# A conformer and latent-attention trunk on one core: scaling order and first taps at the beginning, final norm at the end

## The chip, the cores and the metric

The kernel runs on one core of a Trainium2 chip. The core has TensorE (PE: matrix products and transposes into PSUM; PEld is its weight load), VectorE (DVE), ScalarE (ACT), GpSimd (POOL) and SyncE (SP, which here only issues DMAs). Each engine works through its own instructions in order and waits for others by semaphores. The metric is the time of one execution on the device in microseconds; the time given is the median of several runs.

## The reference, cut to what matters

Two layers over 256 tokens of 2048 channels, all in float32. Layer 0 mixes tokens by a convolution module, layer 1 by latent attention, each is followed by a squared-ReLU MLP, and one RMS norm ends it.

```python
def rms_norm(x, g):
    y = xf * lax.rsqrt(jnp.mean(xf * xf, axis=-1, keepdims=True) + NORM_EPS)
    return (y * g.astype(jnp.float32)).astype(x.dtype)

def conv_module(h, w_pw1, b_pw1, w_dw, b_dw, ln_g, ln_b, w_pw2, b_pw2):
    u = h @ w_pw1 + b_pw1
    a, gate = jnp.split(u, 2, axis=-1)
    u = a * jax.nn.sigmoid(gate)
    u = (causal depthwise convolution of u with w_dw, width 31) + b_dw
    u = jax.nn.silu(layer_norm(u, ln_g, ln_b))
    return u @ w_pw2 + b_pw2

for layer in range(DEPTH):
    h = rms_norm(x, norm_mixer_g[layer])
    x = x + (conv_module(h, ...) if layer % 2 == 0 else mla(h, ...))
    x = x + sq_relu_mlp(rms_norm(x, norm_mlp_g[layer]), mlp_w1[layer], mlp_w2[layer])
return rms_norm(x, final_norm_g)
```

The change touches three places of it: the first `rms_norm` and the first product of `conv_module`, the 31 taps of the first 128 channels, and the last `rms_norm`.

## The kernel before

**Products in two parts.** Every float32 factor is split into a rounded part "hi" and the rest "lo" (`split_half`, L149 to L156). ScalarE rounds (L154: `hi<-raw`), then another engine subtracts (L155: `lo<-raw,hi`). A load of weights ("raw", 1 MB, three buffers) is split in two halves of 128x1024; the hi and lo tiles have six buffers each (`WB`). In the convolution's first product GpSimd does the subtraction, later VectorE does. A product is three matmuls: hi by hi, hi by lo, lo by hi (L482 to L484 in the convolution, L180 to L182 elsewhere).

**The beginning.** The tokens x are loaded to `xs` in four DMAs. VectorE and ScalarE find the mean squares of the two token tiles t, `rsqrt` gives r0. `norm0(n)` scales the 512 channels of block n for both t (two VectorE instructions, L627). `turn0(n)` transposes them on PE (L237, eight transposes), into PSUM tiles of two pools (tr for even n, sum for odd n, two buffers each), and for each 128 channels ScalarE writes the rounded transposed tile (L186) and VectorE its rest (L193). `conv_half(n, h)` splits half h of load n: L154 on ScalarE, L155 on GpSimd. `conv_load(n)` issues load n on SP's queue and waits for a raw buffer, that is for the splits of load n - 3. `conv_mm(c, k0)` is the product of chunk c (128 of the convolution's channels, and as many of the gate) over four blocks of 128 input channels from k0, 24 matmuls; a chunk needs 16 such blocks and two loads. `turn(w_dw ...)` brings the tap weights into place by PE transposes (L276) and VectorE copies (L277). This part stands in `tc.manual_schedule()`: each engine runs its instructions in the order in which the code writes them.

The order written before is: norm0(0), norm0(1), conv_half(0, 0), turn0(0), conv_half(0, 1), conv_load(3), norm0(2), turn0(1), norm0(3), conv_mm(0, 0), turn0(2), both halves of load 1, turn0(3), conv_mm(0, 4), and so on to conv_mm(0, 12).

**The chunks.** For each of 16 chunks `glu` takes a sigmoid on ScalarE (L499) and a product on VectorE (L500) and gives `ub`, 30 columns of padding and 256 tokens. The 31 taps are shared. `pe_taps` does the first three on PE as matmuls with diagonal matrices (L515; the diagonals are made by ScalarE, L506), and ScalarE adds the bias in place (L518). VectorE does the other 28, each one multiply-add into the chunk's PSUM tile (L549). `dve_taps` leaves 16 of them for the next chunk's turn, when VectorE alternates between two chunks. The last two chunks have more taps on PE.

**The end.** `product_A` multiplies by the second MLP matrix in four column blocks of 512. The last block ends with its last three weight loads taken first for token tile 0, then for tile 1, so that tile 0 can be finished while PE works on tile 1. Per tile: `add` (L323) adds the product to `xs`, `prepare` takes squares with their sums on ScalarE (L335), `finish` (L1249) sums the four blocks' squares, takes the inverse root, and scales the four blocks with r and the norm's weights gf in one VectorE instruction each (L1257), each followed by a store issued by SP (L1260).

Of the kernel before, what the change touches and what calls it, by code (L numbers as in the profile page):

```python
# [10 lines left out]
F32 = mybir.dt.float32  # L11
# [3 lines left out]
AF = mybir.ActivationFunctionType  # L15
# [3 lines left out]
P = 128  # L19
D = 2048  # L20
KC = D // P
T = 2
# [12 lines left out]
CHUNK = 64  # L35
HALVES = 2
PAD_CONST = 24
PAD_SMALL = 48
PAD_RIGHT = 48
PAD_KV = 8  # L40
PAD_O = 56
# [31 lines left out]
def trunk_kernel(  # L73
# [54 lines left out]
    def nm(s):  # L128
        uid[0] += 1
        return f"{s}_{uid[0]}"  # L130
# [205 lines left out]

        return ssq, add, prepare

    def product_A(w, k_lo, nk, hi, lo, add, prepare, blocks=range(NNB), due=(), finish=None):


        due = list(due)
        for n in blocks:
            ps = [acc_tile() for _ in range(T)]

            n_end = 3 if finish is not None and n == blocks[-1] else 0
            wjs = []

            def products(u, t):
                for j in range(4):  # L350
                    k = 4 * u + j
                    mm3(ps[t], hi(k, t), lo(k, t), *wjs[u](j), k == 0, k == nk - 1)

            for u in range(nk // 4):
                wjs.append(load_split([rows(w, k_lo + 4 * u, 4, n * NB, NB)], 4))
                if u < nk // 4 - n_end:
                    for j in range(4):
                        k = 4 * u + j
                        for t in range(T):
                            mm3(ps[t], hi(k, t), lo(k, t), *wjs[u](j), k == 0, k == nk - 1)  # L360
                while due:
                    prepare(due.pop(0))
            if n_end:
                for t in range(T):
                    for u in range(nk // 4 - n_end, nk // 4):
                        products(u, t)
                    add(n, ps, t)
                    prepare(n, t)
                    finish(t)
            else:  # L370
                for t in range(T):
                    add(n, ps, t)
                due.append(n)
        while due:
            prepare(due.pop(0))

    def mlp(layer, ssq, next_gain, finish=None):

        with ExitStack() as cx:
            mp = cx.enter_context(tc.tile_pool(name=f"mp{layer}", bufs=1, reuse_waits="tile"))  # L380
            nkh = FF // P // HALVES
            r2 = small.tile([P, T], F32, tag="r2", name=nm("r2"))
            nssq = None
            for hf in range(HALVES):
                hh, hl = [], []
                for g in range(nkh // 4):
                    ps = [acc_tile() for _ in range(4)]
                    c0 = (hf * nkh + 4 * g) * P
                    for u in range(KC // 4):
                        wj = load_split([rows(mlp_w1[layer], 4 * u, 4, c0, NB)], 4)  # L390
                        for j in range(4):
                            k = 4 * u + j
                            wh, wl = wj(j)
                            for b in range(4):
                                bs = slice(b * P, (b + 1) * P)

                                nc.tensor.matmul(ps[b], wh[:, bs], xhl(k), start=k == 0, stop=False)  # L397
                                nc.tensor.matmul(ps[b][:, :S], wl[:, bs], xh(k), start=False, stop=k == KC - 1)  # L398
                    gh = mp.tile([P, 4, S], F32R, tag="gh", name=nm("gh"), bufs=nkh // 4)
                    gl = mp.tile([P, 4, S], F32R, tag="gl", name=nm("gl"), bufs=nkh // 4)  # L400
                    for b2 in range(2):
                        v = mp.tile([P, 2, S], F32, tag="v", name=nm("v"), bufs=2)
                        for b in range(2):
                            o = ps[2 * b2 + b]
                            nc.scalar.activation(v[:, b, :], o[:, S:], AF.Copy)  # L405
                            nc.vector.tensor_tensor(v[:, b, :], o[:, :S], v[:, b, :], op=ALU.add)
                        nc.vector.scalar_tensor_tensor(out=v, in0=v, scalar=0.0, in1=v, op0=ALU.max, op1=ALU.mult)
                        bs = slice(2 * b2, 2 * b2 + 2)
                        nc.scalar.activation(gh[:, bs, :], v, AF.Copy)
                        nc.vector.tensor_tensor(gl[:, bs, :], v, gh[:, bs, :].bitcast(F32), op=ALU.subtract)  # L410
                    hh.append(gh)
                    hl.append(gl)
                if hf == 0:
                    r = rms_rstd(ssq, NNB, D, "n")
                    nc.vector.tensor_tensor(r2, r, r, op=ALU.mult)
                nssq, add, prepare = residual_stage(hf == HALVES - 1, next_gain, r2)
                product_A(
                    mlp_w2[layer],
                    hf * nkh,
                    nkh,  # L420
                    lambda k, t: hh[k // 4][:, k % 4, t * P : (t + 1) * P],
                    lambda k, t: hl[k // 4][:, k % 4, t * P : (t + 1) * P],
                    add,
                    prepare,
                    finish=(lambda t: finish(nssq, t)) if finish is not None and hf == HALVES - 1 else None,
                )
            return nssq


    with ExitStack() as cx:  # L430
# [36 lines left out]
        def conv_split(n):  # L467
            conv_half(n, 0)
            conv_half(n, 1)
# [14 lines left out]
                    nc.tensor.matmul(o, wl[:, bs], xh(k), start=False, stop=k == KC - 1)  # L484

        pss, ubs, pcs, cas, cts = {}, {}, {}, {}, {}
        n_pe = lambda c: PE_TAPS[c % 4] + {KC - 2: PE_MORE[0], KC - 1: PE_MORE[1]}.get(c, 0)
        rest = lambda c: {KC - 2: REST[1], KC - 1: 0}.get(c, REST[0])
        tap = lambda c, w: w_dw[:, w * KC + c : w * KC + c + 1]

# [18 lines left out]
        def pe_taps(c, dgs):  # L509

            pc = pcs[c] = sum_tile()[:, :S]
            for w in range(n_pe(c)):
                if w == len(dgs):
                    dgs.append(diag(c, w))
                nc.tensor.matmul(pc, dgs[w], ubs[c][:, w : w + S], start=w == 0, stop=w == n_pe(c) - 1)  # L515
            left[c] = list(range(n_pe(c), W))
            if c < KC - 1:
                nc.scalar.activation(pc, pc, AF.Identity, bias=b_dw[:, c : c + 1])  # L518
            else:

                pcs[c], last_sum[:] = acc_tile()[:, :S], [pc]

# [7 lines left out]
        def dve_tap(c):  # L530
            w = left[c].pop(0)
            out = pcs[c]
            if last_sum and c == KC - 1:
                if w == n_pe(c):
                    nc.vector.tensor_scalar(
                        out, ubs[c][:, w : w + S], scalar1=tap(c, w), scalar2=b_dw[:, c : c + 1],
                        op0=ALU.mult, op1=ALU.add,
                    )
                    return
                if not left[c]:  # L540
                    half = cv2.tile([P, S], F32, tag="half", name=nm("half"), bufs=1)
                    nc.vector.scalar_tensor_tensor(
# [60 lines left out]
        with tc.manual_schedule():  # L603
# [30 lines left out]
                    to_T(xn, 4 * n + 2 * j, xh, xl, g_mix[0], sum_tile() if n % 2 else None)  # L634


            norm0(0)
            norm0(1)
            conv_half(0, 0)
            turn0(0)  # L640
            conv_half(0, 1)
            conv_load(3)
            pss[0] = [acc_tile() for _ in range(2)]
            norm0(2)
            turn0(1)
            norm0(3)
            conv_mm(0, 0)
            turn0(2)
            conv_split(1)
            turn0(3)  # L650
            conv_mm(0, 4)
            conv_load(4)
            turn(vecs2, vecs2_rows)
            for i in range(4):
                turn(w_dw[:, i * NW : (i + 1) * NW], w_rows[i])
            conv_split(2)
            conv_mm(0, 8)
            conv_mm(0, 12)
            dgs = [diag(0, w) for w in range(n_pe(0))]
            fills = []  # L660
            for c in range(1, KC + 1):
                n = UC * c
# [582 lines left out]
    with tc.tile_pool(name="fin", bufs=1, reuse_waits="tile") as fp:  # L1245
        gf = fp.tile([P, D], F32, name="gf")
        nc.scalar.dma_start(gf, final_norm_g.rearrange("(a n) -> a n", a=1).partition_broadcast(P))

        def finish(ssq, t):  # L1249
            ms = small.tile([P, 1], F32, tag="msf", name=nm("ms"))  # L1250
            nc.vector.tensor_reduce(ms, ssq[:, t, :], axis=AX.X, op=ALU.add)
            nc.vector.tensor_scalar(ms, ms, scalar1=1.0 / D, scalar2=None, op0=ALU.mult)
            r = rsqrt(ms, 1, EPS, "f")
            for n in range(NNB):
                sl = slice(n * NB, (n + 1) * NB)
                ob = xs[:, t, sl]
                nc.vector.scalar_tensor_tensor(  # L1257
                    out=ob, in0=ob, scalar=r, in1=gf[:, sl], op0=ALU.mult, op1=ALU.mult
                )
                nc.sync.dma_start(out[0, t * P : (t + 1) * P, sl], ob)  # L1260

        mlp(1, ssq, None, finish)


_INS = [
# [23 lines left out]
```

## Time and profile before

| what | value |
|---|---|
| median of 3 runs | 2031.42 us (2030.94 to 2032.25) |
| the profiled execution | 2031.51 us |
| its span, first to last instruction | 2029.7 us |
| TensorE busy | 1997.2 us (98%) |
| VectorE, ScalarE, GpSimd busy | 1227.8, 964.5, 174.0 us |
| first product of the convolution (L482) | 15.22 us from the start of the span |
| end of PE's last matmul (wait of L323 ends) | 2020.2 us |
| store issues after it | 2024.41, 2025.07, 2025.73, 2026.40 us |

Times in timelines are microseconds from the start of the span. A row of the timeline has the start, the duration, the engine, the line, the operation, what it writes and reads, and in brackets the idle time of the engine before it and who ended that. "x4" means that four alike were merged. Neighbouring instructions of an engine overlap a little, so the step from one start to the next is shorter than a duration.

### The profile page before, as it was taken

To read this page: it belongs to the slowest core of one execution; us is meant where nothing else is said; L and a number is where in the kernel's file an instruction comes from. 1 tells how busy PE (TensorE), PEld (TensorE's weight loads), DVE (VectorE), ACT (ScalarE), POOL (GpSimd) and SP (SyncE) were. 2 spreads that over 40 slices of the span, in tenths; PEclk is the share of its full clock that TensorE was granted. 3 is DMA by queue.
4 is the path that set the end of the run, shared out by engine and by line. 5 is a ranking of instruction groups with operands and counts; after the bars stand their busy time and mean duration, and the time that the engine had idled before them with its cause. 6 is when DMAs were issued, how large, how long until landed. Compare 5 with 4: busy or idle time off the path is not lost.

```text
span 2029.7 us, 28001 instructions
## 1 busy us (share of the span) xinstructions
PE 1997.2 (98%) x11150; PEld 1749.3 (86%) x11150; DVE 1227.8 (60%) x1858; ACT 964.5 (48%) x1364; POOL 174.0 (9%) x101
## 2 busy tenths in 40 slices
PE   7999999999999999999999899999999999999998
PEld 7999888888888888888898898888888888888886
DVE  5999866665544465555446675665554455565454
ACT  5444665544433354444445564554443334454442
POOL 5887400000000000000000000000000000000000
PEclk9999999999999999999999999999999999999999
DMA  7555355665565666655555335566655566655653
GB/s 235 167 167 166 123 188 174 200 187 187 193 200 187 191 191 193 193 187 188 187 169 171 105 125 168 187 205 188 191 197 192 189 198 192 189 187 190 200 192 104
DMA packets 243267, 367.59 MB, mean 181 GB/s; under 512 B 15416, under 2 KB 89792, under 8 KB 242880
## 3 DMA queue, kind: packets, MB, share of 16 engines
q1 hardware_dynamic: 242400, 364.68, 56.8%
q8 instruction: 87, 1.43, 0.3%
q10 hardware_dynamic: 736, 1.12, 0.2%
q14 instruction: 44, 0.36, 0.1%
HBM read 363.68 MB, written 2.10 MB: 180 GB/s over the span
## 4 chain that ended last, share of the span: by engine, by line
PE 95%; DVE 3%; ACT 1%; issue 0%; DMA 0%; SPq 0%; DVEq 0%; ACTq 0%
PE acc L397 23%; PE acc L180 16%; PE acc L181 16%; PE acc L182 16%; PE acc L398 12%; PE acc L482 3%; PE acc L484 3%; PE acc L483 3%; PE sum L515 1%; PE tr L237 1%; DVE lo L155 1%; DMA xs<-in_x 0%; ACT hi L154 0%; PE acc L1011 0%; PE acc L1012 0%
## 5 line engine op out<-in xcount | busy, mean ns | idle before, releaser
L155 DVE TENSOR_TENSOR lo<-raw,hi 128x1024 fp32r<-128x1024 f32 (+1 forms) x628 | 755.6, 1206 | 682.7 <-ACT hi L154 669.8
L154 ACT ACTIVATE hi<-raw 128x1024 fp32r<-128x1024 f32 (+1 forms) x696 | 722.8, 1046 | 790.2 <-PE acc L181 453.8
L397 PE MATMUL acc<-xt,hi 128*128 128x512 f32 x2048 | 710.6, 390 | 0.0
L398 PE MATMUL acc<-xt,lo 128*128 128x256 f32 x2048 | 577.7, 282 | 0.0
L397 PEld LDWEIGHTS acc<-xt,hi 128*128 128x128 f32 x2048 | 384.3, 188 | 80.5
L180 PE MATMUL acc<-hi,gh 128*128 128x512 f32 x1024 | 398.6, 389 | 0.0
L182 PE MATMUL acc<-lo,gh 128*128 128x512 f32 x1024 | 398.4, 389 | 0.0
L181 PE MATMUL acc<-hi,gl 128*128 128x512 f32 x1024 | 398.4, 389 | 0.0
L398 PEld LDWEIGHTS acc<-xt,lo 128*128 128x128 f32 x2048 | 387.1, 189 | 0.1
L182 PEld LDWEIGHTS acc<-lo,gh 128*128 128x128 f32 x1024 | 192.2, 188 | 40.2
L180 PEld LDWEIGHTS acc<-hi,gh 128*128 128x128 f32 x1024 | 192.2, 188 | 40.0
L181 PEld LDWEIGHTS acc<-hi,gl 128*128 128x128 f32 x1024 | 192.2, 188 | 39.3
L549 DVE SCALAR_TENSOR_TENSOR sum<-ub,w_dw,sum 128x256 f32<-128x256 f32 x402 | 167.6, 483 | 4.9 <-ACT sum L518 2.9
L155 POOL TENSOR_TENSOR lo<-raw,hi 128x1024 fp32r<-128x1024 f32 x68 | 161.9, 2404 | 57.7 <-ACT hi L154 57.7
L482 PE MATMUL acc<-xt,hi 128*128 128x256 f32 x512 | 147.4, 288 | 0.0
L484 PE MATMUL acc<-xt,lo 128*128 128x256 f32 x512 | 143.1, 280 | 0.4 <-POOL lo L155 0.4
L483 PE MATMUL acc<-xt,hi 128*128 128x256 f32 x512 | 143.1, 280 | 0.0
L483 PEld LDWEIGHTS acc<-xt,hi 128*128 128x128 f32 x512 | 96.3, 188 | 0.6 <-DVE xt L193 0.2
L484 PEld LDWEIGHTS acc<-xt,lo 128*128 128x128 f32 x512 | 96.2, 188 | 0.6 <-POOL lo L155 0.6
L482 PEld LDWEIGHTS acc<-xt,hi 128*128 128x128 f32 x512 | 96.3, 188 | 0.4
L918 POOL MEMSET pad_kv<- 128x8 f32 x1 | 0.1, 105 | 772.6 <-PE acc L182 772.6
L405 ACT ACTIVATE v<-acc 128x256 f32<-128x256 f32 x128 | 46.4, 381 | 25.3 <-PE acc L398 25.3
(215 smaller groups left out, 1772.8 us busy)
## 6 DMA issues: line engine op xcount, KB each, us to landing
raw<-in_mlp_w SPq DMA_DIRECT2D x256, 1024.0 KB, 5.2
raw<-in_conv_w_pw SPq DMA_DIRECT2D x64, 512.0 KB, 5.1
raw<-in_conv_w_pw SPq DMA_DIRECT2D x16, 1024.0 KB, 5.2
raw<-in_mla_w_o SPq DMA_DIRECT2D x16, 1024.0 KB, 5.3
raw<-in_mla_w_kv_up SPq DMA_DIRECT2D x8, 1024.0 KB, 5.6
raw<-in_mla_w_in SPq DMA_DIRECT2D x8, 576.0 KB, 3.7
raw<-in_mla_w_in SPq DMA_DIRECT2D x4, 1024.0 KB, 5.6
raw<-in_mla_w_q_up SPq DMA_DIRECT2D x16, 256.0 KB, 3.3
```

The lines of the kernel that those rows point to most:

```text
L154: nc.scalar.activation(hi, raw[:, js, :], AF.Copy)
L155: eng.tensor_tensor(lo, raw[:, js, :], hi.bitcast(F32), op=ALU.subtract)
L180: nc.tensor.matmul(ps, sh, mh, start=start, stop=False)
L181: nc.tensor.matmul(ps, sl, mh, start=False, stop=False)
L182: nc.tensor.matmul(ps, sh, ml, start=False, stop=stop)
L397: nc.tensor.matmul(ps[b], wh[:, bs], xhl(k), start=k == 0, stop=False)
L398: nc.tensor.matmul(ps[b][:, :S], wl[:, bs], xh(k), start=False, stop=k == KC - 1)
L405: nc.scalar.activation(v[:, b, :], o[:, S:], AF.Copy)
L482: nc.tensor.matmul(o, wh[:, bs], xh(k), start=k == 0, stop=False)
L483: nc.tensor.matmul(o, wh[:, bs], xl(k), start=False, stop=False)
L484: nc.tensor.matmul(o, wl[:, bs], xh(k), start=False, stop=k == KC - 1)
L549: nc.vector.scalar_tensor_tensor(out=out, in0=ubs[c][:, w : w + S], scalar=tap(c, w), in1=pcs[c], op0=ALU.mult, op1=ALU.add)
```

## The change

At the beginning, all four `norm0` are written ahead of everything else; the first half of load 1 is split before conv_mm(0, 0) and `turn0(2)`, the second half between `turn0(2)` and `turn0(3)`; the tap weights' turns come one conv_mm later. Chunk 0 has no taps on PE: VectorE does all 31, the first with the bias. At the end, after the first weight load of the last column block, a new function `before` sums the squares of the first three blocks into `part` and multiplies these blocks of `xs` by the norm's weights. `finish` then adds only the last block's squares, multiplies the last block by the weights while ScalarE takes the root, and scales the four blocks by the inverse root alone: blocks 0 and 2 on VectorE with stores from SP's queue, 1 and 3 on ScalarE with stores from its own queue. `PAD_SMALL` makes room for the additional small tiles.

```diff
-PAD_SMALL = 48
+PAD_SMALL = 32
...
+                if u == 0 and n_end:
+                    before()
...
-        n_pe = lambda c: PE_TAPS[c % 4] + {KC - 2: PE_MORE[0], KC - 1: PE_MORE[1]}.get(c, 0)
+        n_pe = lambda c: 0 if c == 0 else PE_TAPS[c % 4] + {KC - 2: PE_MORE[0], KC - 1: PE_MORE[1]}.get(c, 0)
...
-            if c < KC - 1:
+            if 0 < c < KC - 1:
                 nc.scalar.activation(pc, pc, AF.Identity, bias=b_dw[:, c : c + 1])
-            else:
+            elif c:
...
-            if last_sum and c == KC - 1:
-                if w == n_pe(c):
-                    nc.vector.tensor_scalar(
-                        out, ubs[c][:, w : w + S], scalar1=tap(c, w), scalar2=b_dw[:, c : c + 1],
-                        op0=ALU.mult, op1=ALU.add,
-                    )
-                    return
+            if c in (0, KC - 1) and w == n_pe(c):
+                nc.vector.tensor_scalar(
+                    out, ubs[c][:, w : w + S], scalar1=tap(c, w), scalar2=b_dw[:, c : c + 1],
+                    op0=ALU.mult, op1=ALU.add,
+                )
+                return
+            if c == KC - 1:
...
-            norm0(0)
-            norm0(1)
+            for n in range(NNB):
+                norm0(n)
             conv_half(0, 0)
             turn0(0)
             conv_half(0, 1)
             conv_load(3)
             pss[0] = [acc_tile() for _ in range(2)]
-            norm0(2)
             turn0(1)
-            norm0(3)
+            conv_half(1, 0)
             conv_mm(0, 0)
             turn0(2)
-            conv_split(1)
+            conv_half(1, 1)
             turn0(3)
             conv_mm(0, 4)
             conv_load(4)
             turn(vecs2, vecs2_rows)
+            conv_mm(0, 8)
             for i in range(4):
                 turn(w_dw[:, i * NW : (i + 1) * NW], w_rows[i])
             conv_split(2)
-            conv_mm(0, 8)
             conv_mm(0, 12)
-            dgs = [diag(0, w) for w in range(n_pe(0))]
+            dgs = []
...
+        def gained(t, n):
+            sl = slice(n * NB, (n + 1) * NB)
+            nc.vector.tensor_tensor(xs[:, t, sl], xs[:, t, sl], gf[:, sl], op=ALU.mult)
+
         def finish(ssq, t):
-            ms = small.tile([P, 1], F32, tag="msf", name=nm("ms"))
-            nc.vector.tensor_reduce(ms, ssq[:, t, :], axis=AX.X, op=ALU.add)
-            nc.vector.tensor_scalar(ms, ms, scalar1=1.0 / D, scalar2=None, op0=ALU.mult)
-            r = rsqrt(ms, 1, EPS, "f")
...
+            nc.vector.tensor_scalar(v, ssq[:, t, n : n + 1], scalar1=1.0 / D, scalar2=part[t], op0=ALU.mult, op1=ALU.add)
+            nc.scalar.activation(w, v, AF.Sqrt)
+            nc.vector.tensor_tensor(xs[:, t, sl], xs[:, t, sl], gf[:, sl], op=ALU.mult)
+            nc.vector.reciprocal(y, w)
+            nc.vector.scalar_tensor_tensor(out=q, in0=y, scalar=v, in1=y, op0=ALU.mult, op1=ALU.mult)
+            nc.vector.tensor_scalar(q, q, scalar1=-0.5, scalar2=1.5, op0=ALU.mult, op1=ALU.add)
+            nc.vector.tensor_tensor(y, y, q, op=ALU.mult)
             for n in range(NNB):
-                sl = slice(n * NB, (n + 1) * NB)
-                ob = xs[:, t, sl]
-                nc.vector.scalar_tensor_tensor(
-                    out=ob, in0=ob, scalar=r, in1=gf[:, sl], op0=ALU.mult, op1=ALU.mult
-                )
-                nc.sync.dma_start(out[0, t * P : (t + 1) * P, sl], ob)
+                ob = xs[:, t, n * NB : (n + 1) * NB]
+                if n % 2:
+                    nc.scalar.activation(ob, ob, AF.Copy, scale=y)
+                else:
+                    nc.vector.tensor_scalar(ob, ob, scalar1=y, scalar2=None, op0=ALU.mult)
+                (nc.scalar if n % 2 else nc.sync).dma_start(out[0, t * P : (t + 1) * P, n * NB : (n + 1) * NB], ob)
+
+        part = []
+
+        def before(ssq):
+            for t in range(T):
+                m = small.tile([P, 1], F32, tag="msp", name=nm("msp"))
+                nc.vector.tensor_reduce(m, ssq[:, t, : NNB - 1], axis=AX.X, op=ALU.add)
+                nc.vector.tensor_scalar(m, m, scalar1=1.0 / D, scalar2=EPS, op0=ALU.mult, op1=ALU.add)
+                part.append(m)
+                for n in range(NNB - 1):
+                    gained(t, n)
+
+        mlp(1, ssq, None, finish, before)
```

More of the change, by code (lines that the diff above doesn't have):

```diff
@@ L337, in residual_stage, with product_A @@
         return ssq, add, prepare
-    def product_A(w, k_lo, nk, hi, lo, add, prepare, blocks=range(NNB), due=(), finish=None):
+    def product_A(w, k_lo, nk, hi, lo, add, prepare, blocks=range(NNB), due=(), finish=None, before=None):
         due = list(due)
@@ L375, in product_A, with mlp @@
             prepare(due.pop(0))
-    def mlp(layer, ssq, next_gain, finish=None):
+    def mlp(layer, ssq, next_gain, finish=None, before=None):
         with ExitStack() as cx:
@@ L425, in mlp @@
                     finish=(lambda t: finish(nssq, t)) if finish is not None and hf == HALVES - 1 else None,
+                    before=lambda: before(nssq),
                 )
@@ L1253, in finish @@
-            r = rsqrt(ms, 1, EPS, "f")
-            for n in range(NNB):
-                sl = slice(n * NB, (n + 1) * NB)
-                ob = xs[:, t, sl]
-                nc.vector.scalar_tensor_tensor(
-                    out=ob, in0=ob, scalar=r, in1=gf[:, sl], op0=ALU.mult, op1=ALU.mult
-                )
-                nc.sync.dma_start(out[0, t * P : (t + 1) * P, sl], ob)
-        mlp(1, ssq, None, finish)
+            n = NNB - 1
+            sl = slice(n * NB, (n + 1) * NB)
+            v = small.tile([P, 1], F32, tag="msf", name=nm("ms"))
@@ new lines, in finish @@
+            w = small.tile([P, 1], F32, tag="wsf", name=nm("ws"))
+            y = small.tile([P, 1], F32, tag="ysf", name=nm("ys"))
+            q = small.tile([P, 1], F32, tag="qsf", name=nm("qs"))
+            nc.vector.tensor_scalar(v, ssq[:, t, n : n + 1], scalar1=1.0 / D, scalar2=part[t], op0=ALU.mult, op1=ALU.add)
+            nc.scalar.activation(w, v, AF.Sqrt)
+            nc.vector.tensor_tensor(xs[:, t, sl], xs[:, t, sl], gf[:, sl], op=ALU.mult)
+            nc.vector.reciprocal(y, w)
```

## The prediction

> **What bounds the kernel now.** I read the page first: busy time by engine, then the chain that ended last.
>
> ```profile
> PE 1997.2 (98%) x11150; PEld 1749.3 (86%) x11150; DVE 1227.8 (60%) x1858; ACT 964.5 (48%) x1364; POOL 174.0 (9%) x101
> PE 95%; DVE 3%; ACT 1%; issue 0%; DMA 0%; SPq 0%; DVEq 0%; ACTq 0%
> ```
>
> TensorE (PE) is busy for 1997.2 of 2029.7 us, so an edit pays only where it moves PE: in the 32.5 us of gaps, or in PE work that goes away. The timeline puts the gaps that matter here in two places: the first 23 us, and the 9.5 us after the last matmul. Then the timeline of the start (start, duration, engine, line, what came before it):
>
> ```profile
> 12.43 1.68 DVE L627 TENSOR_SCALAR xn<-xs,y 128x512 f32<-128x512 f32 x4
> 13.84 2.49 POOL L155 TENSOR_TENSOR lo<-raw,hi 128x1024 fp32r<-128x1024 f32 x1 [12.46 <-ACT hi L154]
> 15.06 1.66 DVE L193 SCALAR_TENSOR_TENSOR xt<-tr,vecs,xt 128x256 fp32r<-128x256 f32 x4 [0.95 <-PE sum L237]
> 15.60 0.38 PE L483 MATMUL acc<-xt,hi 128*128 128x256 f32 x1
> 16.39 0.39 PE L484 MATMUL acc<-xt,lo 128*128 128x256 f32 x1 [0.40 <-POOL lo L155]
> 16.64 0.48 DVE L627 TENSOR_SCALAR xn<-xs,y 128x512 f32<-128x512 f32 x1
> 16.78 2.59 POOL L155 TENSOR_TENSOR lo<-raw,hi 128x1024 fp32r<-128x1024 f32 x1 [0.45 <-ACT hi L154]
> 17.03 2.63 DVE L627 TENSOR_SCALAR xn<-xs,y 128x512 f32<-128x512 f32 x1
> 19.71 0.98 PE L237 MATMUL tr<-ident,xn 128*128 128x128 f32 x7 [0.35 <-DVE xn L627]
> 21.76 1.29 PE L237 MATMUL sum<-ident,xn 128*128 128x128 f32 x8 [1.07 <-DVE xn L627]
> 22.81 0.37 PE L482 MATMUL acc<-xt,hi 128*128 128x256 f32 x1
> ```
>
> The reader should see one thing above all. A scaling (L627) takes 0.48 us, each starting 0.40 after the last. The one at 17.03 took 2.63, ending 0.29 after GpSimd's split (16.78 + 2.59 = 19.37). So these two exclude each other. And GpSimd, which asked at 16.78 in the middle of the scaling of 16.64, went ahead of the next scaling, although that followed at once.
>
> **The change, start.** All eight scalings now precede VectorE's first L193. Nothing delays GpSimd: its first split waits for ScalarE's rounding (L154), which waits for a DMA, not for VectorE. So I replay the rows with the rule just read (times from the start of the span):
> - Scalings 1 to 4: 12.43 to 14.1 as before. GpSimd asks at 13.84 and goes ahead of scaling 5, which waits for 13.84 + 2.49 = 16.33 and ends 0.29 later, 16.62. Scaling 6 starts 0.08 before that end, 16.54.
> - Split 2 asks at 16.78, as before, again inside a scaling (6). Taking the step from the scaling's start to the split's end from the rows (19.37 - 16.64 = 2.73), it ends at 19.27; scaling 7 ends at 19.56, scaling 8 asks at 19.48.
> - Split 3 is the moved one (conv_half(1, 0)). ScalarE ends its four L186 at 18.0, rounds in 1.07, so it is ready at 19.2 and waits behind split 2. It asks inside scaling 7 (port effectively taken at 19.08) and goes ahead of scaling 8: end 19.08 + 2.73 = 21.81. Scaling 8 ends at 22.1.
> - First L193 at 22.0; L483 stood 0.54 after it (15.06, 15.60), so it runs at 22.56 instead of 15.60: **6.96 us late**. PE is in order, so everything is behind it.
>
> Given back: PE's waits between 15.60 and 22.81 vanish, as splits and scalings are then long done: for the split 15.60 to 16.39 less one step of 0.12, 0.67; for the scalings 0.57 and 1.48 (the step lengths around 19.71 and 21.76, less 0.11 a transpose). 6.96 - 2.72 = **+4.2 us**. The moved ScalarE roundings cost nothing: split 4 then ends near 33, and the third quarter's products only begin after 34; without that cover it would be a split of 2.4 us.
>
> The stall also costs clock. The next rows are stretches in the attention stage (length, busy us and instructions per engine, granted clock, DMA share):
>
> ```profile
> 1123.20:1126.60 3.40, 3.40 (x31) 3.40 (x30) 3.37 (x7) 1.12 (x2) 0.00 (x0) 1.00 0.15 45
> 1126.60:1130.00 3.40, 1.90 (x17) 1.67 (x16) 2.11 (x11) 1.19 (x5) 0.00 (x0) 1.00 0.68 154
> 1130.00:1133.40 3.40, 3.40 (x18) 3.40 (x18) 2.34 (x7) 1.36 (x2) 0.00 (x0) 0.50 0.02 5
> ```
>
> A stretch of 3.4 us in which PE was busy 56% was followed by half clock for a fully busy 3.4 us. A stall of 7 us holds such a stretch whatever its phase, so products start again at half clock: 0.213 us a step (18 matmuls in the row of half clock against 31 in the first, and the 14 warm-up transposes at 9.60 took 3.25) against 0.117. If a stretch under 56% busy does not raise it, half clock lasts 1.9 to 5.3 us of work and loses half, 0.95 to 2.65. On this profile's phase (its clock record steps where stretches end, here at 20.65, 24.07, 27.48; the one to 24.07 would be 44% busy) 23 products lose 2.2. Bounds: 0 and 2.65; I take **+2.0**, near this phase.
>
> The Trainium skill (TensorE: Matmul & The Clock Gate, Part 1) says a whole free-running window of about 3.4 us of sustained activity is needed to release the gate; by that rule the loss is an estimated 1.7 to 3.4 us and the sum some 0.5 larger. The trace agrees with the length, and does not show what a window busy at 44% does.
>
> **First chunk's taps.** Gone from PE: the six matmuls of three taps.
>
> ```profile
> 34.11 0.28 PE L484 MATMUL acc<-xt,lo 128*128 128x256 f32 x1
> 34.23 1.47 PE L515 MATMUL sum<-ub,dg 128*128 128x256 f32 x6
> 35.35 0.47 PE L482 MATMUL acc<-xt,hi 128*128 128x256 f32 x1
> ```
>
> 34.11 to 35.35 less one step: **-1.1 us**. VectorE does 15 taps instead of 12 before the next chunk, 3 x 0.53 = 1.6, but no longer waits 2.25 for L518; it then idled 3.5 us for the sigmoid, which hides it. Without that slack the 1.6 would count. Later chunks leave VectorE 0.6 to 0.8 idle and PE none, so PE's shift stays. The w_dw turns moved past conv_mm(0, 8): five turns took 25.80 to 27.14, and one of their waits for a copy goes: **-0.2** (0 to -0.4). Load 4 on SP's queue waits for split 4 (33 instead of 27.6), for a rounding needed after 40: nothing.
>
> **The end.** The weights' six early multiplications (0.69 each, row L410) and four small steps, 4.8 us, fall where VectorE splits 1.23 of every 2.72 us and ScalarE waits for PE to free one of six halves, so a split is five halves (13 us) ahead: nothing; 4.8 uncovered. The last column block:
>
> ```profile
> 2023.63 2.74 DVE L1257 SCALAR_TENSOR_TENSOR xs<-xs,y,gf 128x512 f32<-128x512 f32 x4
> 2026.40 0.33 SPq L1260 DMA_DIRECT2D out<-xs  x1
> 2026.50:2027.00 0.50, 0.00 (x0) 0.00 (x0) 0.00 (x0) 0.00 (x0) 0.00 (x0) 0.50 1.09 369
> ```
>
> The new chain saves two small steps and pays 0.61 of multiplication under a root of 0.42: 0.2 earlier. The first piece is ready after 0.48 instead of 0.75, so its store issues at 23.95 instead of 24.41. ScalarE's pieces cost 0.63 each (row L335) and its issues 0.44 (ACTq rows at the start), so the last issue is at 25.2 instead of 26.40. But the stores already fill the DMA engines (share 1.09), 1 MB in 3.1 us: the end moves with the first store and a little denser queue. **-0.7** (0 if the stores pack worse, -1.2 if the last issue decides).
>
> **Sum.** +4.2 +2.0 -1.1 -0.2 -0.7 = +4.2. The profiled execution took 2031.51 (span 2029.7 and 1.8 around it), 0.1 over the median 2031.42, so about 2035.7.
>
> **Rivals.**
> - *VectorE keeps the port through its eight scalings.* For it: GpSimd asks only once, 0.2 before scaling 5. Against: the row of 17.03. Scalings end at 15.7, split 1 at 18.0; L484 then waits 1.65 longer, the later waits (2.05) go: -0.4 -0.2 -1.1 -0.7 = -2.4, **2029.1**. This is the case of not slower; it decides if scaling 5 is 0.48 long.
> - *Scaling 8 slips in before split 3.* For it: they ask within 0.05 us of each other's release. Against: so did 17.03 and 16.78. L483 at 20.4: 4.8 - 2.7 = +2.1, clock 0 to 1.7, the rest -2.0: +0.1 to +1.8, **2032.5**.
> - *The clock does not fall, or rises at 24.07.* 0 to 0.7 instead of 2.0: +2.2 to +2.9, **2034.1**. Against: the rows of 1126.60 and 1130.00.
> - *Half clock lasts a further window (1.7), or the stall feeds a second one:* +6, **2037.5** or more. Nothing in the rows asks for it.
>
> **Chances.** Forecast 0.62, clock kept 0.12, VectorE first 0.12, slip 0.08, longer half clock 0.06. Range: I leave out VectorE first and the last (0.18), so from the slip's lower end, less 0.4 by which single runs lie under the median, 2031.2, to the forecast's upper bounds, 4.2 + 2.65 - 1.1 and no other gain, 2037.3. A change under 0.2% (4.1 us) is about what a measurement of this kernel can't tell from none: the bound, 2035.5, cuts the forecast's own range (2034.3 to 2037.3), some 0.7 of it above: 0.62 x 0.7 + 0.06 = 0.50 slower. Faster needs 2027.3, which all savings together at their best (-2.4, with the end at -1.2 and the turns at -0.4: -3.1) miss: 0.04. Same: 0.46.
>
> **What would show it.** Scaling 5 near 2.6 us and 7 or 8 again; first L193 near 22.0 and L483 near 22.6; product steps of 0.213 after it; no L515 before chunk 1; the first products of chunk 1 some 6 us later than before, chunk 2's some 5; last store issue near 1.2 earlier relative to the last matmul, the end 0.7. Eight scalings of 0.48 in a row, or L193 before 18, would make it wrong.

## The result, and the profile after

| | before | changed |
|---|---|---|
| median of 19 runs | 2031.95 us | 2036.03 us |
| range of the runs | 2030.94 to 2033.14 | 2033.26 to 2036.92 |
| profiled execution, its span | 2031.51, 2029.7 | 2036.42, 2034.6 |

The changed kernel is slower by a ratio of 1.0018 (95% interval 1.0011 to 1.0024). The medians differ by 4.1 us, the profiled executions by 4.9. Some lines moved by three: L485 to L487 in the changed kernel are L482 to L484 before, L630 is L627, L502 is L499.

First the timeline of the start in the changed kernel, VectorE and GpSimd, then PE (start, duration, engine, line; rows of a kind are merged differently from stretch to stretch, so a row of scalings can cover others that follow):

```profile
12.53 9.55 DVE L630 TENSOR_SCALAR xn<-xs,y 128x512 f32<-128x512 f32 x8
...
13.93 2.50 POOL L155 TENSOR_TENSOR lo<-raw,hi 128x1024 fp32r<-128x1024 f32 x1 [12.55 <-ACT hi L154]
14.12 2.98 DVE L630 TENSOR_SCALAR xn<-xs,y 128x512 f32<-128x512 f32 x2
16.71 2.60 POOL L155 TENSOR_TENSOR lo<-raw,hi 128x1024 fp32r<-128x1024 f32 x1 [0.28 <-ACT hi L154]
17.03 2.57 DVE L630 TENSOR_SCALAR xn<-xs,y 128x512 f32<-128x512 f32 x1
17.03 5.05 DVE L630 TENSOR_SCALAR xn<-xs,y 128x512 f32<-128x512 f32 x2
19.27 2.52 POOL L155 TENSOR_TENSOR lo<-raw,hi 128x1024 fp32r<-128x1024 f32 x1
22.00 0.86 DVE L193 SCALAR_TENSOR_TENSOR xt<-tr,vecs,xt 128x256 fp32r<-128x256 f32 x2
22.52 0.58 PE L486 MATMUL acc<-xt,hi 128*128 128x256 f32 x1 [7.01 <-DVE xt L193]
...
23.33 0.41 PE L486 MATMUL acc<-xt,hi 128*128 128x256 f32 x1
23.55 0.41 PE L487 MATMUL acc<-xt,lo 128*128 128x256 f32 x1
...
27.43 1.03 PE L237 MATMUL tr<-ident,xn 128*128 128x128 f32 x8
28.30 1.04 PE L237 MATMUL sum<-ident,xn 128*128 128x128 f32 x8
29.09 0.37 PE L485 MATMUL acc<-xt,hi 128*128 128x256 f32 x1
```

Eight scalings of 0.48 us, 0.40 apart, would take 3.3; they take 9.55. The fifth starts at 14.12, just after GpSimd's first split began at 13.93, and it and the sixth last 2.98 together; the seventh takes 2.57, and with the eighth 5.05. So the fifth, the seventh and the eighth are the slow ones, and each ends 0.3 us after one of GpSimd's three splits. (What the two engines cannot use at the same time is called the port, here and in the prediction.) PE waits 7.01 for that L193 and then steps 0.21 a matmul (23.33 to 23.55) until 27.2.

Then the stretches between the clock's steps (length, busy us and instructions of PE, PEld, DVE, ACT, POOL, granted clock, DMA share):

```profile
13.52:16.93 3.41, 1.98 (x17) 1.78 (x16) 3.41 (x4) 3.13 (x8) 2.72 (x2) 1.00 0.73 217
16.93:20.35 3.42, 0.00 (x0) 0.00 (x0) 3.42 (x3) 2.11 (x5) 3.42 (x2) 1.00 0.96 273
20.35:23.76 3.41, 1.24 (x6) 1.24 (x6) 3.41 (x6) 0.00 (x0) 1.44 (x1) 0.50 1.02 325
23.76:27.18 3.42, 3.42 (x18) 3.42 (x18) 1.45 (x4) 0.00 (x0) 0.00 (x0) 0.50 1.06 328
27.18:30.59 3.41, 3.41 (x32) 3.41 (x32) 1.66 (x4) 2.53 (x6) 0.00 (x0) 1.00 0.05 15
```

The idle stretch (16.93 to 20.35) is followed by half clock; the stretch to 23.76, 36% busy, did not raise it; the fully busy one to 27.18 did.

Last, the end of the changed kernel (the last block of token tile 1):

```profile
2025.70 0.75 DVE L323 SCALAR_TENSOR_TENSOR xs<-acc,r,xs 128x512 f32<-128x512 f32 x1 [4.17 <-PE acc L182]
...
2028.80 1.33 ACT L1273 ACTIVATE xs<-xs,ys 128x512 f32<-128x512 f32 x2 [1.11 <-DVE ys L1269]
2028.80 0.88 DVE L1275 TENSOR_SCALAR xs<-xs,ys 128x512 f32<-128x512 f32 x2
2029.31 0.81 SPq L1276 DMA_DIRECT2D out<-xs  x2
2029.55 0.95 ACTq L1276 DMA_DIRECT2D out<-xs  x2
```

And one half microsecond after them, in the columns of the stretches above:

```profile
2031.50:2032.00 0.50, 0.00 (x0) 0.00 (x0) 0.00 (x0) 0.00 (x0) 0.00 (x0) 0.50 1.09 356
```

All four stores are issued within 1.2 us (2029.31 to 2029.55 + 0.95), and the DMA engines are full after them (share 1.09), as they were before.

The same work in both traces shows where the 4.9 us lie:

| landmark | before | changed | difference | of which new |
|---|---|---|---|---|
| products of block 4 begin | 22.81 | 29.09 | +6.28 | +6.28 |
| sigmoid of chunk 0 | 33.03 | 39.19 | +6.16 | -0.12 (turns) |
| sigmoid of chunk 1 | 45.54 | 50.39 | +4.85 | -1.31 (taps) |
| sigmoid of chunk 15 | 225.57 | 229.92 | +4.35 | -0.50 |
| start of the last adds of MLP 0's third block | 998.48 | 1002.84 | +4.36 | 0 |
| first add after the attention | 1267.73 | 1273.17 | +5.44 | +1.08 |
| last L323 | 2020.26 | 2025.70 | +5.44 | 0 |
| end of the span | 2029.69 | 2034.61 | +4.92 | -0.52 (end) |

### The profile page after: what moved, and what is told of

It reads as the page before. It is cut to its first block, busy times and chain, and to the rows that moved or that the text cites. A ratio compares the mean times of both kernels' runs of the same rounds, so it can differ in the third digit from the quotient of the medians.

```text
span 2034.6 us, 27980 instructions
## 1 busy us (share of the span) xinstructions
PE 1997.4 (98%) x11144; PEld 1750.8 (86%) x11144; DVE 1233.5 (61%) x1863; ACT 965.8 (47%) x1364; POOL 174.1 (9%) x101
## 4 chain that ended last, share of the span: by engine, by line
PE 95%; DVE 3%; ACT 1%; issue 1%; DMA 0%; SPq 0%; ACTq 0%; DVEq 0%
PE acc L399 23%; PE acc L182 16%; PE acc L180 16%; PE acc L181 16%; PE acc L400 12%; PE acc L486 3%; PE acc L485 3%; PE acc L487 3%; PE sum L518 1%; PE tr L237 1%; DVE lo L155 1%; DMA xs<-in_x 0%; ACT hi L154 0%; PE acc L1014 0%; PE tr L1097 0%
## 5 line engine op out<-in xcount | busy, mean ns | idle before, releaser
L486 PE MATMUL acc<-xt,hi 128*128 128x256 f32 x512 | 144.2, 282 | 7.0 <-DVE xt L193 7.0
L485 PE MATMUL acc<-xt,hi 128*128 128x256 f32 x512 | 148.0, 289 | 0.0
L487 PE MATMUL acc<-xt,lo 128*128 128x256 f32 x512 | 143.9, 281 | 0.0
L486 PEld LDWEIGHTS acc<-xt,hi 128*128 128x128 f32 x512 | 97.4, 190 | 7.6 <-DVE xt L193 7.2
L485 PEld LDWEIGHTS acc<-xt,hi 128*128 128x128 f32 x512 | 97.3, 190 | 0.4
L487 PEld LDWEIGHTS acc<-xt,lo 128*128 128x128 f32 x512 | 97.2, 190 | 0.0
```

Source lines behind the costliest of these rows:

```text
L485: nc.tensor.matmul(o, wh[:, bs], xh(k), start=k == 0, stop=False)
L486: nc.tensor.matmul(o, wh[:, bs], xl(k), start=False, stop=False)
```

## The experiments

Each kernel was timed beside the kernel before on the same chip, whose medians there were 2031.87 (first four), 2032.19 (next four) and 2031.68 (last three). The changed kernel was not among them: "under the changed kernel" compares bare medians, and taking each against the kernel before that ran beside it moves these differences by up to 0.3 us. The code shown is cut to the lines that matter.

**The order alone.** The kernel before with the changed order of the beginning, nothing else.

```diff
-            norm0(0)
-            norm0(1)
+            for n in range(NNB):
+                norm0(n)
...
+            conv_half(1, 0)
             conv_mm(0, 0)
```

> The kernel before with the new order of the beginning alone (scalings first, the moved split halves, the tap weights' turns later); the taps of chunk 0 and the end as before. Theory (GpSimd goes ahead of waiting scalings, PE stalls, clock falls): scalings 5, 7 and 8 take about 2.6 us, first L193 at 22.0, L483 at 22.5, chunk 0's sigmoid 6 us later than before; +5.5 to +6.5 us over before. Rival (the order costs little, the slower time comes from the taps or the end): within 1 us of before.

Measured: 2037.17 us (2034.59 to 2038.09), ratio 1.0023 (1.0014 to 1.0032), +5.3 us, 0.2 short of the range expected. The loss is the order's, and the order alone is 1.1 slower than the whole change. Its profiled execution took 2035.84 and shows another path, the rival that the prediction called the slip, though not for the reason given there. DVE and GpSimd in it:

```profile
16.52 0.87 DVE L627 TENSOR_SCALAR xn<-xs,y 128x512 f32<-128x512 f32 x2
17.06 2.52 POOL L155 TENSOR_TENSOR lo<-raw,hi 128x1024 fp32r<-128x1024 f32 x1 [0.76 <-ACT hi L154]
17.31 2.56 DVE L627 TENSOR_SCALAR xn<-xs,y 128x512 f32<-128x512 f32 x1
19.79 1.65 DVE L193 SCALAR_TENSOR_TENSOR xt<-tr,vecs,xt 128x256 fp32r<-128x256 f32 x4
37.13 0.48 ACT L499 ACTIVATE sg<-acc,vecs 128x256 f32<-128x256 f32 x1 [1.10 <-PE acc L484]
```

Split 2 asked at 17.06 instead of 16.71, when scaling 7 was already running, so only the eighth waited for it, and L193 begins at 19.79. In this execution the record of the granted clock first rises at 15.09, not 13.52, so PE's first transposes were slower and ScalarE's rounding for split 2 came later. The other profiles bear this out: in the ten in which the work up to split 2 is the same, it starts 4.18 us after the first scaling where the clock first rose at 12.2 to 13.5 us (six), 4.35 in the kernel before (13.83), and 4.53 to 4.65 where it rose at 14.7 to 15.3 (three). The sigmoid of chunk 0 (last row) is +4.1 over before instead of +6.2. So the race between the second split and the seventh scaling has two outcomes some 2 us apart. The changed kernel's 19 runs lie in two groups, 6 from 2033.26 to 2034.43 and 13 from 2035.75 to 2036.92; that these are the two outcomes fits, but is not shown, as no execution of the lower group has been profiled.

**The taps alone, and the end alone.**

```diff
-        n_pe = lambda c: PE_TAPS[c % 4] + {KC - 2: PE_MORE[0], KC - 1: PE_MORE[1]}.get(c, 0)
+        n_pe = lambda c: 0 if c == 0 else PE_TAPS[c % 4] + {KC - 2: PE_MORE[0], KC - 1: PE_MORE[1]}.get(c, 0)
```

> The kernel before with chunk 0's 31 taps on VectorE alone. Theory: PE loses six matmuls, VectorE's 1.6 us more is hidden by its wait for the next sigmoid: -1.1 us (-0.7 to -1.8, as the profile after gained some 0.5 more over the later chunks). Rival (VectorE is the bound of the chunks, the three taps come back at the end of them): 0 to +1.6 us.

Measured: 2030.27 us (2029.46 to 2032.49), ratio 0.9992 (0.9984 to 1.0001), -1.6 us. The sign by the timing is just short of sure; the trace shows the mechanism: the sigmoids of chunks 0 and 1 are 11.20 us apart instead of 12.51, with no wait of PE between. So -1.31 at once, 1.12 for the matmuls and 0.19 at the change between shapes.

```profile
32.92 0.47 ACT L499 ACTIVATE sg<-acc,vecs 128x256 f32<-128x256 f32 x1 [4.61 <-PE acc L484]
44.12 0.47 ACT L499 ACTIVATE sg<-acc,vecs 128x256 f32<-128x256 f32 x1 [6.05 <-PE acc L484]
```

> The kernel before with the new end alone. Theory: -0.5 us, the stores' transfer rate sets the end, the early multiplications are hidden. Rival 1 (the last store's issue sets the end): -1.7 us. Rival 2 (the early multiplications hold up the splits): above 0.

```diff
+                if u == 0 and n_end:
+                    before()
...
-                nc.sync.dma_start(out[0, t * P : (t + 1) * P, sl], ob)
+                (nc.scalar if n % 2 else nc.sync).dma_start(out[0, t * P : (t + 1) * P, n * NB : (n + 1) * NB], ob)
```

Measured: 2030.95 us (2030.57 to 2032.95), ratio 0.9996 (0.9987 to 1.0005), -0.9 us by the medians, which the interval does not tell from nothing and which alone excludes neither rival. The trace does: the last matmul is 8.96 us before the end of the span, against 9.47, so -0.5 and not -1.7; and from the first add after the attention to the last L323 both kernels take 752.53 us, so the early multiplications hold nothing up.

**All but the order.** The changed kernel with the old order of the beginning (between these lines all is as before the change).

```diff
-            for n in range(NNB):
-                norm0(n)
+            norm0(0)
+            norm0(1)
             conv_half(0, 0)
...
+            norm0(2)
             turn0(1)
-            conv_half(1, 0)
+            norm0(3)
             conv_mm(0, 0)
```

> The changed kernel with the old order of the beginning. Theory (the parts add up): -1.1 - 0.5 = -1.6 us against before, some 6 us faster than the changed kernel. Rival (the parts need each other): not faster than before.

Measured twice: 2029.56 us, ratio 0.9988 (0.998 to 0.9997), and beside the last kernels 2030.56, ratio 0.999 (0.9981 to 0.9999). The parts other than the order gain 1.1 to 2.3 us, and taking the order back makes the changed kernel 5.5 to 6.5 faster.

> The same kernel as all_but_order, beside two_forms on one chip: 2029.5 us, -1.5 to -3 against before.

The second came out 1.0 above the figure expected and 0.4 short of the gain's near bound, so single medians here are good to about 1 us. Part of that can be seen in the two profiles of this one kernel: the attention (from the last adds of MLP 0's third block to the first add after it) takes 269.20 us in one, with half clock for two stretches, and 270.40 in the other, with half clock for three.

**The stall filled.** 60 transposes that nothing reads, while PE waits.

```diff
             conv_half(1, 0)
+            keep_warm(ident, 60, warm_pt)
             conv_mm(0, 0)
```

> The changed kernel with 60 transposes of the identity on PE between turn0(1)'s transposes and conv_mm(0, 0): 60 x 0.11 = 6.6 us, from 15.1 to some 21.7, into a tile that nothing reads. They end before L483 can run (22.5), so they add no wait. Theory (the stall also costs clock): the products start again at 0.117 a step, chunk 0's sigmoid comes 2.2 us earlier than in the profile after; -1.8 to -2.2 us against the changed kernel, +2 against before. Rival (the clock costs nothing): equal to the changed kernel, +4 against before.

Measured: 2033.82 us (2033.11 to 2034.41), ratio 1.0008 (1.0 to 1.0017): 2.2 under the changed kernel, and all its runs lie in a range of 1.3 us. In its timeline the scalings and L193 are where they were, and the matmuls step 0.12:

```profile
12.51 9.61 DVE L631 TENSOR_SCALAR xn<-xs,y 128x512 f32<-128x512 f32 x8
15.20 6.71 PE L220 MATMUL acc<-ident 128*128 128x128 f32 x60
22.57 0.39 PE L487 MATMUL acc<-xt,hi 128*128 128x256 f32 x1 [0.53 <-DVE xt L193]
22.79 0.28 PE L488 MATMUL acc<-xt,lo 128*128 128x256 f32 x1
22.91 0.28 PE L486 MATMUL acc<-xt,hi 128*128 128x256 f32 x1
37.13 0.47 ACT L503 ACTIVATE sg<-acc,vecs 128x256 f32<-128x256 f32 x1 [3.96 <-PE acc L488]
```

The sigmoid of chunk 0 is 2.06 earlier than in the changed kernel (39.19). Useless work on PE saves 2 us: this stall costs its length and, besides, the clock.

**The splits held back.** GpSimd copies a column of the eighth scaling's result first, which makes its first split wait (`PAD_SMALL` is 24, for the additional tile).

```diff
+            held = small.tile([P, 1], F32, tag="held", name="held", bufs=1)
+            nc.gpsimd.tensor_copy(held, xn[:, 1, D - 1 : D])
             conv_half(0, 0)
             turn0(0)
```

> The changed kernel in which GpSimd first copies one column of the eighth scaling's result, so that its first split waits for all scalings: the order that the change describes, in fact. Theory (the port is the only cause of the start's loss): eight scalings of 0.48, first L193 at 15.7, first split 15.8 to 18.2, L484 at 18.3, the products of block 4 at 22.4; -0.4 -0.2 -1.1 -0.5 = -2.2 us against before, 6.3 under the changed kernel. Rival (the moved turns or another queue hold PE too): no more than 4 us under the changed kernel.

Measured: 2031.12 us (2029.94 to 2032.06), ratio 0.9994 (0.9986 to 1.0003): 4.9 under the changed kernel, but 1.1 short of the forecast against before. Its timeline:

```profile
12.40 3.26 DVE L630 TENSOR_SCALAR xn<-xs,y 128x512 f32<-128x512 f32 x8
15.57 1.65 DVE L193 SCALAR_TENSOR_TENSOR xt<-tr,vecs,xt 128x256 fp32r<-128x256 f32 x4
15.95 7.02 POOL L155 TENSOR_TENSOR lo<-raw,hi 128x1024 fp32r<-128x1024 f32 x3
18.36 0.38 PE L487 MATMUL acc<-xt,lo 128*128 128x256 f32 x1 [1.87 <-POOL lo L155]
```

Its stretches between the clock's steps:

```profile
16.23:19.65 3.42, 1.55 (x12) 1.36 (x13) 2.66 (x7) 2.68 (x6) 3.42 (x2) 1.00 0.87 250
19.65:23.06 3.41, 3.41 (x19) 3.41 (x18) 0.00 (x0) 0.00 (x0) 3.32 (x2) 0.50 1.04 303
```

Held apart, eight scalings take 3.26 us and L193 comes at 15.57: running beside the splits is the cause of the 9.55. But PE then waits for the first split until 18.36, so a stretch was only 45% busy, and half clock followed for 3.4 us, which loses half of them, 1.7. Block 4's products begin at 24.28, 1.9 later than forecast.

**Held and filled.** The same with 28 transposes in that wait.

```diff
             conv_half(1, 0)
+            keep_warm(ident, 28, warm_pt)
             conv_mm(0, 0)
```

> splits_held with 28 transposes of the identity on PE before conv_mm(0, 0): 28 x 0.11 = 3.1 us, from 15.0 to 18.1, where PE waits for the first split until 18.3. Theory (splits_held missed its forecast by 1.1 us because PE, idle for most of a 3.4 us stretch, fell to half clock at 19.6): the products stay at 0.117 a step, block 4 starts at 22.5 instead of 24.3; -1.1 to -1.7 us against splits_held. Rival (the clock's fall there is chance, or the rest is a wait behind the moved turns): within 0.4 us of splits_held.

Measured: 2030.12 us (2029.13 to 2030.91), ratio 0.999 (0.9981 to 0.9998). That is 1.0 under splits_held by the bare medians, just short of what the theory expected, and only 0.5 when each is taken against the kernel before on its own chip (-1.6 and -1.1), so the times do not decide between theory and rival. The trace does:

```profile
23.10 0.36 PE L486 MATMUL acc<-xt,hi 128*128 128x256 f32 x1
```

Block 4's products begin at 23.10, 10.35 after the first scaling, against 11.88 in splits_held: 1.5 earlier, with no half clock at the start. In the kernel before it is 10.38, so even with the wait filled, eight scalings in a row bring block 4 no earlier: the first product that needs a split (18.75) comes 2.04 later against the first scaling than before, as much as the 2.05 of waits that go. The 0.4 that the forecast of splits_held had counted there did not come.

**Scalings that take one port.**

```diff
-                        scalar1=r0[:, t : t + 1], scalar2=None, op0=ALU.mult,
+                        scalar1=r0[:, t : t + 1], scalar2=0.0, op0=ALU.mult, op1=ALU.add,
+                        accum_out=sums0[:, t * NNB + n : t * NNB + n + 1],
```

> The changed kernel with each scaling written so that it also gives its sum (a second scalar of 0 added, accumulator output, which nothing reads); same result in xn. Theory (the scaling excludes GpSimd because it takes both of VectorE's ports in its fast form): this form runs at about 0.7 us and does not wait for splits: last scaling ends at 17.5 to 18, first L193 at 17.5, L483 at 18.1; -1.5 to -2.5 us against before. Rival (any VectorE instruction on SBUF alone is held by a split): scalings of 2.6 us again, as the changed kernel.

Measured: 2030.04 us (2029.0 to 2032.04), ratio 0.9993 (0.9984 to 1.0002), 6.0 under the changed kernel in the same order of code. From its timeline:

```profile
13.96 0.74 DVE L632 TENSOR_SCALAR_CACHE_REDUCE xn<-xs,y 128x512 f32<-128x512 f32 x1
14.03 2.37 POOL L155 TENSOR_TENSOR lo<-raw,hi 128x1024 fp32r<-128x1024 f32 x1 [12.65 <-ACT hi L154]
14.62 0.74 DVE L632 TENSOR_SCALAR_CACHE_REDUCE xn<-xs,y 128x512 f32<-128x512 f32 x1
17.96 1.66 DVE L193 SCALAR_TENSOR_TENSOR xt<-tr,vecs,xt 128x256 fp32r<-128x256 f32 x4
18.49 0.39 PE L486 MATMUL acc<-xt,hi 128*128 128x256 f32 x1 [1.96 <-DVE xt L193]
```

The scalings in a slower form (0.74 instead of 0.48) that runs beside the split end four microseconds earlier than those in the fast one that waits for it. The L193 and the products come 0.4 later than expected. The Trainium skill (SBUF — State Buffer, Who interferes with whom) says that tensor_scalar can take the port pair shared with GpSimd, except in the form that also writes out its accumulator; the trace agrees with both halves: 2.57 us beside a split in the one form, 0.74 in the other.

**The end on one engine.** All four last scalings on VectorE, all stores from SP.

```diff
-                if n % 2:
-                    nc.scalar.activation(ob, ob, AF.Copy, scale=y)
-                else:
-                    nc.vector.tensor_scalar(ob, ob, scalar1=y, scalar2=None, op0=ALU.mult)
-                (nc.scalar if n % 2 else nc.sync).dma_start(out[0, t * P : (t + 1) * P, n * NB : (n + 1) * NB], ob)
+                nc.vector.tensor_scalar(ob, ob, scalar1=y, scalar2=None, op0=ALU.mult)
+                nc.sync.dma_start(out[0, t * P : (t + 1) * P, n * NB : (n + 1) * NB], ob)
```

> The changed kernel with all four last scalings on VectorE and all stores from SP. Pieces every 0.40 us, last store issue about 1.2 after the first (1.05 in the profile after, which uses two engines). Theory (the transfers set the end): time from the last matmul to the end within 0.3 us of the changed kernel's 8.95. Rival (two engines and two queues are the gain): 0.5 us or more longer, as long as before's 9.47.

Measured: 2035.85 us (2033.7 to 2036.74), ratio 1.0019 (1.001 to 1.0027); the last matmul is 8.98 us before the end, against 8.95 in the changed kernel.

```profile
2029.24 1.81 SPq L1273 DMA_DIRECT2D out<-xs  x4
```

The last store is issued 0.6 us later in it (5.11 after the last matmul instead of 4.50) and the end does not move. From the issue of the first store to the end it takes 5.28 us in the kernel before, 5.29 in the changed one and 5.27 here: the transfers set the end, and it moves with the first store. The second engine and the second queue gain nothing.

**Two forms.** The best of these: the first four scalings in the fast form, ahead of the first split; the last four in the one-port form after the first four L193 (`norm0` has both forms, by block; only the order is shown).

```diff
+            norm0(0)
+            norm0(1)
             conv_half(0, 0)
             turn0(0)
             conv_half(0, 1)
...
+            norm0(2)
+            norm0(3)
             turn0(1)
             conv_half(1, 0)
```

> The changed kernel with the scalings of blocks 0 and 1 first in the fast form (before GpSimd asks), and those of blocks 2 and 3 in the form with a sum after turn0(0)'s L193, before turn0(1)'s. Theory: L193 at 15.1 as before, the four later scalings at 0.7 us each end at 19.4 beside the splits, PE's waits of 2.05 us before block 4 shrink to under 0.3: block 4's products at 20.9 instead of 22.8; -1.5 to -2 us against all_but_order, 2027.5 to 2028.5. Rival (the summing form is held by a split too, or the later L193 hold block 4): not faster than all_but_order.

Measured: 2028.3 us (2027.45 to 2028.65), ratio 0.9981 (0.9972 to 0.999), 3.4 us under the kernel before, 7.7 under the changed one and 2.3 under all_but_order on the same chip, a little more than the 2 expected. Block 4's products begin at 21.30 instead of 22.81, 0.4 later than expected.

```profile
12.42 1.67 DVE L634 TENSOR_SCALAR xn<-xs,y 128x512 f32<-128x512 f32 x4
14.88 1.66 DVE L193 SCALAR_TENSOR_TENSOR xt<-tr,vecs,xt 128x256 fp32r<-128x256 f32 x4 [0.78 <-PE sum L237]
16.45 0.74 DVE L636 TENSOR_SCALAR_CACHE_REDUCE xn<-xs,y 128x512 f32<-128x512 f32 x1
20.92 0.63 PE L237 MATMUL sum<-ident,xn 128*128 128x128 f32 x4 [0.15 <-DVE xt L193]
21.30 0.36 PE L485 MATMUL acc<-xt,hi 128*128 128x256 f32 x1
```

After its first product PE no longer waits for a scaling at all; the 0.15 left before the last four transposes is a wait for L193, which reads the PSUM tiles that they need.

## Why the prediction was right, point by point

- **The replay of the port.** Right, nearly to the step: the fifth scaling slow with the first split, the seventh and eighth with the second and third; L193 at 22.00 as predicted, L483 (now L486) at 22.52 against 22.56. splits_held and scalings_one_port show that it is the exclusion by the splits and not the order of VectorE's work: both keep that order, and both lose the stall. That GpSimd goes ahead of the scaling that follows at once was read from one row; the three slow scalings after repeat it.
- **Half clock.** The step of 0.213 and the fall were right. Forecast +2.0, or 2.2 on the profile's phase; stall_filled gives 2.2 by the medians and 2.06 in the trace. That the phase of the changed kernel's profile (first rise at 13.52) lay near that of the profile before (13.83) was luck: over all profiles the first rise lies anywhere from 12.2 to 15.3. The stretch of 36% did not raise the clock, so the rival in which it rises early falls.
- **Given back.** +4.2 and +2.0 against +6.28 measured at block 4.
- **Taps.** The mechanism was right and the size small: -1.1 forecast, -1.31 measured, because the changes between shapes go too. The other 0.5, over chunks 1 to 15 (most take 12.74 us, those of 12.81 or more are six before and one after), is not shown to come from the taps: all_but_order, profiled twice, takes 179.45 and 179.86 us from chunk 1's sigmoid to chunk 15's, against 180.03 in the kernel before and 179.53 in the changed one, and end_only, with the old taps, 179.67.
- **Turns.** -0.2 forecast, -0.12 measured.
- **The end.** -0.7 forecast, -0.52 measured. The first store's issue came 0.53 earlier relative to the last matmul (0.46 forecast), and the end moved with it; the "denser queue" that made up the rest of the 0.7 did not come. The last store is issued 1.67 earlier, not 1.2: ScalarE started its second piece before its first store was issued. That this bought nothing follows from the reason the prediction gave, full DMA engines; tail_one_engine shows it.
- **Not in the sum.** The attention took 1.08 us longer in the profiled execution, with half clock for three stretches instead of two. One and the same kernel (all_but_order, profiled twice) took 269.20 us there with two and 270.40 with three, so nothing shows that this is the change's. Without it and without the 0.5 of the chunks, the profiles' rows that are the change's add up to +6.28 -0.12 -1.31 -0.52 = +4.3, against +4.2 forecast, so the terms were right, or wrong by 0.2 at most, one by one. That the medians are 4.1 apart is closer than the forecast had earned: if the lower group of runs is the other outcome of the race, a third of the executions did not take the path that was priced.
- **The chances.** The lower bound of the forecast's own range, 2034.3, does not follow from its terms: at their low ends (+4.2 +0.95 -1.1 -0.4 -1.2) they give 2034.0. And with 19 runs a side a change a little under 0.2% could be told from none: the interval of the ratio, 1.0011 to 1.0024, does not hold 1.
- **The slip**, given 0.08, was seen in one profile, of the order alone, for another reason (a late split 2). Its stall and clock were put at 2.1 plus 0 to 1.7; that profile shows +4.1 at chunk 0's sigmoid, with half clock for two stretches, 0.3 more than the bound. If 6 of the 19 runs took it, 0.08 was too little.

## What to carry to other kernels

When two engines exclude each other, moving one's work "ahead" in the code moves nothing of the other's: ask when the other one's inputs are ready, and which goes first when both wait. A form of the instruction that is slower alone and does not exclude the neighbour is worth trying beside a change of the order: the fastest kernel here uses both. Price a PE stall of several microseconds at its length plus the half clock after it, and test that with idle work on PE.

## What the runs showed of the hardware that was not expected

A stall need not be complete to cost clock: a stretch 45% busy (16.23 to 19.65 in splits_held) was followed by half clock. The busy share alone does not decide it: in the kernel before a stretch busy for 1.52 of 3.40 us (1116.30 to 1119.70) kept full clock, and the prediction's stretch of 56% did not. Nor does most of a stretch raise it again: in the changed kernel's attention a stretch in which PE was busy for 2.69 of 3.40 us did not.

```profile
1143.30:1146.70 3.40, 2.69 (x13) 2.62 (x13) 3.36 (x7) 2.62 (x5) 0.00 (x0) 0.51 0.71 262
1146.70:1150.10 3.40, 3.40 (x18) 3.40 (x17) 1.47 (x6) 1.80 (x6) 0.00 (x0) 0.50 0.59 167
```

The phase of these stretches against the start of the kernel differs from one profile to the next (first rise at 12.2 to 15.3 us). It moves the start of split 2, and in the four profiles with the new order, the plain form of the scaling and nothing held back, the slow scalings go by it: the fifth, seventh and eighth in the three with a rise at 12.5 to 13.5, the fifth and eighth in the one with 15.09. That the two groups of the run times come from this is likely, but not shown.
